# A hybrid attention block on one core: weights' neighbours reordered, gates kept ahead, branch sums added in DRAM

## The chip, the cores and the metric

The kernel runs on one NeuronCore of a Trainium2 chip. The core has TensorE (PE in the profile, with its weight loads as PEld), VectorE (DVE), ScalarE (ACT), GpSimd (POOL) and SyncE (SP), which run side by side and meet at semaphores; data comes from DRAM by DMA, issued here by SP, ACT and POOL. TensorE writes its sums to PSUM, which has eight banks. The metric is the device time of one execution in microseconds, as the median of several runs.

## The reference, cut to what matters

The input is 512 tokens of width 2048. One RMSNorm feeds one wide projection; its columns are split among three branches and three gates. All is float32.

```python
h = rms_norm(x, norm_g);  proj = h @ w_in
conv_y = b_gate * causal_depthwise_conv(c_gate * u, conv_w)          # 1024 channels
o_conv = (conv_y * silu(conv_z)) @ w_conv_out
mla_y  = mla_attention(...)      # 16 heads: low-rank q and kv, QK-norm, rotary part, block-causal mask
o_mla  = (mla_y * silu(mla_z)) @ w_mla_out
mem_y  = memory_attention(...)   # 4 heads of width 256 over 256 memory tokens, QK-norm
o_mem  = (mem_y * silu(mem_z)) @ w_mem_out
merged = sigmoid(g_conv) * o_conv + sigmoid(g_mla) * o_mla + sigmoid(g_mem) * o_mem
x = x + merged @ w_o
```

## The kernel before

Every product is made of three matmuls: an operand is split into a rounded part and its remainder (`split`, `weights`, `pair_split`: a copy on ScalarE gives the high half `whi`, a subtraction on VectorE the low half `wlo`), and `mm3` (L158 to L163) multiplies high by high, high by low, low by high.

Two kinds of product share one stream of weights. Dense products (`dense_units`) step through a weight matrix in chunks of two blocks of 128 rows; a unit is one `mm3`. Panel products (`panels`, `panel_steps`) use seven products in place of eight (Strassen's scheme in Winograd's form) on pairs of blocks: a weight chunk is loaded as four quarters, `pair_weights` adds four sums to them (L263 to L265), then splits seven; the moving side is prepared the same way by `pair_sums` (L243 to L246) and `pair_split` (L249, L250). A panel has four chunks, its first two panels are interleaved so that the fourth chunks, which need pairs 6 and 7, come last.

`queue` holds the weight chunks of all products in the order of their use, and `take` (L172) hands out the next one. When chunk c is taken, the halves of chunk c+1 are made and chunk c+2 is loaded (with `ahead=2` one further each). Raw weights have three buffers, halves two; in the first stage a third pair of buffers (`staged_parts`) serves every third chunk.

The stages follow each other so: keys and values of the memory (32 steps, during which x is scaled and its pairs made), the main projection `w_h` in 60 panels, 8 rounds of heads two at a time, the convolution's output product, the memory attention, `w_mla_out` in 8 panels, `w_mem_out` as dense product, and `w_o` in 8 panels.

TensorE's order is that of the program text. In the rounds of heads the text is interleaved by strings: `ORDER_KV` and `ORDER_Q` say after how many units of the projection for the next pair of heads (`w`) a step of an attention stream follows. `A` and `B` are the older pair's two streams, `a` and `b` the newer's. A stream's steps are: transposes of keys, of queries, of the rotary part (first head of a pair only), four blocks of scores with softmax, four of transposed probabilities, and the product with the values. `ORDER_MEM` does the same for four memory heads. SP's order is that of the text, too. The order on VectorE, ScalarE and POOL comes from a planner with simulated times, except where `manual_schedule` says that it is the text's: for VectorE this holds for the first six panel chunks of the main projection.

Gates are computed in the main projection and kept in DRAM (`gdram`). Where an output product ends, its banks are multiplied by the gate. `conv_result` writes the first branch's share to `mgdram`, `finish_mla` adds the second's by an accumulating DMA, and `mem_pair` (L1231) does the third: it loads gate and sum into one buffer `mg`, multiplies (L1236), adds (L1237), and makes the pair for `w_o` (`pair_parts`).

Of the kernel before, what the change touches and what calls it, by code (L numbers as in the profile page):

```python
# [30 lines left out]
P = 128  # L31
# [20 lines left out]
ORDER_KV = "2w B B B w B w A 6w B w B B B 5w"  # L52
ORDER_Q = "a a a B a a a 4w a w b b 5w a 4w a w a a w"
ORDER_KV1 = "16w"
ORDER_Q1 = "4w a a 2w a 2w a a a w a w b b 4w a w a w a a"
ORDER_LAST = "a a a B a a a 4w a w b b", "5w a 4w a w a a w"
ORDER_TAIL = "b b b b a 7w b w b b b 4w b"
ORDER_MEM = "0 0 4w 1 1 4w 0 0 2 2w 1 1 3 3w 0 0 2 2 w 1 1 3 3 2w 2 2 3w 3 3 w 2 2 3 3"
# [49 lines left out]
def body(ctx, tc, a, out):  # L108
# [165 lines left out]
    def panel_steps(xp, e, tag, middle=None, tail=None):  # L274
# [235 lines left out]
    def staged_parts():  # L510
# [7 lines left out]
    parts_of_x = all_parts()  # L518
    for grp in range(4):
# [43 lines left out]
    for _ in parts_of_x:  # L563
        pass
    close_st()
# [76 lines left out]
    def rotary():  # L642
# [76 lines left out]
        def turned(tag):  # L719
# [4 lines left out]
            nc.gpsimd.dma_start(krdram, kr)  # L724
        later.append(turned)
        yield
# [288 lines left out]

# [365 lines left out]
```

## Time and profile before

| what | us |
|---|---|
| median of 3 runs (lowest, highest) | 2192.47 (2190.98, 2194.52) |
| the profiled execution | 2187.3 |
| its span from first to last instruction | 2185.5 |
| TensorE busy | 2128.3 |
| VectorE busy | 1741.5 |
| ScalarE busy | 1003.8 |

The mean granted clock of TensorE over the span is 0.992. A row of a group of instructions reads: line, engine, operation, output and inputs by the program's names, shapes, count, then total busy time in us and the mean of one in ns, then idle time of the engine before them and what ended it. A row of waits reads: who waited, for whom, us in total, times, the longest. L12 is line 12 of the kernel before.

### The profile page before, as it was taken

The numbers are of one execution on the slowest core, as the hardware profiler recorded it, in microseconds if no ns is written. First come the engines' busy times: TensorE is split into PE (matmuls) and PEld (weight loads), VectorE is DVE, ScalarE is ACT, GpSimd is POOL, SyncE is SP. The second block draws the span as 40 slices with busy tenths as digits, with TensorE's granted clock in tenths as the row PEclk, the third lists the DMA queues.
The fourth block names the chain that finished last, engine by engine and source line by source line (L and its number), as shares of the span: only waits on it lengthen the run. The fifth ranks groups of instructions, "written<-read, shape, count | busy, mean of one in ns | idle before, by whom it ended". The sixth has DMA issues, their size and how long they took to land.

```text
span 2185.5 us, 38852 instructions
## 1 busy us (share of the span) xinstructions
PE 2128.3 (97%) x16040; PEld 2038.7 (93%) x16040; DVE 1741.5 (80%) x2764; ACT 1003.8 (46%) x1219; POOL 123.9 (6%) x173
## 2 busy tenths in 40 slices
PE   9989999999999999999999999999999999998799
PEld 8789999999999999999999999888888799987799
DVE  6986888888888888888888786888877688757787
ACT  6743444344334334444444444877764433323333
POOL 0000000000000000000000001221211100000000
PEclk9999999999999999999999999999999999999899
DMA  8633433333334334343444446222266765554343
GB/s 331 231 106 136 155 136 126 126 126 129 123 126 137 115 129 137 118 141 127 136 136 139 133 136 244 74 82 108 98 231 249 306 186 173 170 204 149 126 147 136
DMA packets 92289, 334.31 MB, mean 153 GB/s; under 512 B 10768, under 2 KB 11024, under 8 KB 90064
## 3 DMA queue, kind: packets, MB, share of 16 engines
q1 hardware_dynamic: 72000, 256.77, 34.4%
q0 software_dynamic: 11616, 51.12, 6.6%
q10 hardware_dynamic: 8496, 23.94, 3.1%
q8 instruction: 125, 2.05, 0.4%
q14 instruction: 52, 0.43, 0.1%
HBM read 273.34 MB, written 58.46 MB: 152 GB/s over the span
## 4 chain that ended last, share of the span: by engine, by line
PE 81%; DVE 8%; DMA 4%; issue 4%; ACT 2%; POOL 0%; SPq 0%; DVEq 0%; POOLq 0%; ACTq 0%
PE acc L161 14%; PE acc L162 14%; PE acc L163 14%; PE aux L163 11%; PE aux L162 11%; PE aux L161 11%; DVE wlo L269 3%; DMA raw<-in_w_mla_out 1%; DMA raw<-in_w_o 1%; DVE raw L263 1%; PE aux L978 1%; DMA sb<-gdram 1%; DMA raw<-in_w_h 1%; PE aux L961 1%; DVE wlo L155 0%
## 5 line engine op out<-in xcount | busy, mean ns | idle before, releaser
L268 ACT ACTIVATE whi<-raw 128x1792 fp32r<-128x1792 f32 x304 | 517.7, 1703 | 793.0 <-PE acc L162 352.8
L269 DVE TENSOR_TENSOR wlo<-raw,whi 128x1792 fp32r<-128x1792 f32 x304 | 614.3, 2021 | 194.2 <-ACT whi L268 193.7
L163 PE MATMUL aux<-xp,wlo 128*128 128x256 f32 (+1 forms) x1712 | 479.5, 280 | 5.0 <-DVE wlo L269 5.0
L161 PE MATMUL aux<-xp,whi 128*128 128x256 f32 (+1 forms) x1712 | 479.8, 280 | 1.0 <-ACT whi L268 1.0
L162 PE MATMUL aux<-xp,whi 128*128 128x256 f32 (+1 forms) x1712 | 480.0, 280 | 0.0
L163 PE MATMUL acc<-xp,wlo 128*128 128x256 f32 x1680 | 469.4, 279 | 3.4 <-DVE wlo L269 3.4
L162 PE MATMUL acc<-xp,whi 128*128 128x256 f32 x1680 | 469.8, 280 | 0.0
L161 PE MATMUL acc<-xp,whi 128*128 128x256 f32 x1680 | 469.3, 279 | 0.0
L163 PEld LDWEIGHTS aux<-xp,wlo 128*128 128x128 f32 (+1 forms) x1712 | 320.4, 187 | 5.6 <-DVE wlo L269 5.6
L161 PEld LDWEIGHTS aux<-xp,whi 128*128 128x128 f32 (+1 forms) x1712 | 321.4, 188 | 1.4 <-ACT whi L268 1.4
L162 PEld LDWEIGHTS aux<-xp,whi 128*128 128x128 f32 (+1 forms) x1712 | 320.9, 187 | 0.0
L163 PEld LDWEIGHTS acc<-xp,wlo 128*128 128x128 f32 x1680 | 314.6, 187 | 4.3 <-DVE wlo L269 4.2
L161 PEld LDWEIGHTS acc<-xp,whi 128*128 128x128 f32 x1680 | 315.6, 188 | 0.0
L162 PEld LDWEIGHTS acc<-xp,whi 128*128 128x128 f32 x1680 | 315.1, 188 | 0.0
L263 DVE TENSOR_TENSOR raw<-raw 128x512 f32<-128x512 f32 x304 | 208.0, 684 | 57.3 <-DMA raw<-in_w_h 29.8
L155 DVE TENSOR_TENSOR wlo<-raw,whi 128x1024 fp32r<-128x1024 f32 (+2 forms) x91 | 101.5, 1119 | 47.7 <-ACT whi L154 47.7
L154 ACT ACTIVATE whi<-raw 128x1024 fp32r<-128x1024 f32 (+2 forms) x91 | 88.9, 977 | 102.6 <-PE acc L162 41.5
L265 DVE TENSOR_TENSOR raw<-raw 128x256 f32<-128x256 f32 x304 | 127.7, 421 | 6.2
L264 DVE TENSOR_TENSOR raw<-raw 128x256 f32<-128x256 f32 x304 | 127.6, 420 | 5.7
L343 POOL TENSOR_TENSOR rs_r<-rs_t,mhalf 128x2 f32<-128x2 f32 (+2 forms) x71 | 69.5, 989 | 270.0 <-DVE rs_t L342 209.6
L161 PE MATMUL acc<-whi,blk 128*128 128x384 f32 (+1 forms) x224 | 84.8, 379 | 0.0
L163 PE MATMUL acc<-whi,blk 128*128 128x384 f32 (+1 forms) x224 | 80.9, 361 | 0.0
(359 smaller groups left out, 3900.9 us busy)
## 6 DMA issues: line engine op xcount, KB each, us to landing
raw<-in_w_h SPq DMA_DIRECT2D x240, 512.0 KB, 3.5
raw<-in_w_mla_out SPq DMA_DIRECT2D x32, 512.0 KB, 3.9
raw<-in_w_o SPq DMA_DIRECT2D x32, 512.0 KB, 3.7
raw<-in_w_mem_kv SPq DMA_DIRECT2D x31, 512.0 KB, 7.2
gdram<-e ACTq DMA_DIRECT2D x22, 512.0 KB, 2.8
raw<-in_w_ukv SPq DMA_DIRECT2D x16, 512.0 KB, 5.6
raw<-in_w_conv_out SPq DMA_DIRECT2D x16, 512.0 KB, 9.0
aadram<-z POOLq DMA_DIRECT2D x8, 896.0 KB, 4.1
```

The costliest lines, as they stand in the source:

```text
L154: act.activation(hi[:, cols], raw[:, cols], AF.Copy)
L155: vec.tensor_tensor(out=lo[:, cols], in0=raw[:, cols], in1=r32(hi[:, cols]), op=ALU.subtract)
L161: nc.tensor.matmul(o, lhsT=s[0], rhs=m[0], start=start, stop=False, skip_group_check=shared)
L162: nc.tensor.matmul(o, lhsT=s[0], rhs=m[1], start=False, stop=False, skip_group_check=shared)
L163: nc.tensor.matmul(o, lhsT=s[1], rhs=m[0], start=False, stop=stop, skip_group_check=shared)
L263: vec.tensor_tensor(out=f[:, 4:6], in0=f[:, 1:3], in1=f[:, 0:1].to_broadcast([P, 2, 256]), op=ALU.add)
L264: vec.tensor_tensor(out=f[:, 6], in0=f[:, 5], in1=f[:, 1], op=ALU.add)
L265: vec.tensor_tensor(out=f[:, 7], in0=f[:, 6], in1=f[:, 3], op=ALU.add)
L268: act.activation(hi, f[:, 1:8], AF.Copy)
L269: vec.tensor_tensor(out=lo, in0=f[:, 1:8], in1=r32(hi), op=ALU.subtract)
L343: pool.tensor_tensor(out=r, in0=t, in1=mhalf[:, :n], op=ALU.pow)
L961: nc.tensor.matmul(sb[:, :n], lhsT=qr[:, cols], rhs=krh[:, :n], start=False, stop=False)
```

## The change

- In the first stage the third pair of buffers serves chunks 0, 3, 6 and so on in place of 2, 5, 8; one more step uses `ahead=2`; one more raw chunk is loaded after the stage; VectorE's order is the text's from step 27 on until the sixth panel chunk.
- `take` can now carry other work: a list `fills`, of which one entry runs behind each chunk's weights. The x pairs 6 and 7 are made there, and in `w_o` the last two merged pairs and the results of a finished panel (`finish_o`).
- A panel's `middle` (loads for its end) stands at chunk 1 in front of its weights, not at chunk 2 behind them; the gate `sg` is loaded by POOL, not SP.
- In `rotary` the transposes of the shared key are put off by one step.
- The first three steps of a new pair of heads stand two units in front of the end of the keys' and values' product, not behind it; `ORDER_Q1` and `ORDER_MEM` are shifted by a few units.
- The convolution's gates are loaded a group ahead (`gate_blocks` is called on its own), and `my` has four buffers, not two.
- The third branch: gates lie in three places inside the tile of pair 7; the products with the gate stand right behind a group's matmuls (`gated`) and are added to `mgdram` by an accumulating DMA; the merged sum is loaded later (`merged`, partly into the tiles of pairs 5 and 6), and its sums and its split stand at fixed steps of the product (`steps_out`). VectorE's order is the text's from there until the ninth panel chunk of `w_o`.

```diff
-ORDER_KV = "2w B B B w B w A 6w B w B B B 5w"
-ORDER_Q = "a a a B a a a 4w a w b b 5w a 4w a w a a w"
+ORDER_KV = "2w B B B w B w A 6w B w B B B 3w a a a 2w"
+ORDER_Q = "B a a a 4w a w b b 5w a 4w a w a a w"
 ORDER_KV1 = "16w"
-ORDER_Q1 = "4w a a 2w a 2w a a a w a w b b 4w a w a w a a"
-ORDER_LAST = "a a a B a a a 4w a w b b", "5w a 4w a w a a w"
+ORDER_Q1 = "6w a a w a 2w a a a w a w b b 3w a w a w a a"
+ORDER_LAST = "B a a a 4w a w b b", "5w a 4w a w a a w"
-ORDER_MEM = "0 0 4w 1 1 4w 0 0 2 2w 1 1 3 3w 0 0 2 2 w 1 1 3 3 2w 2 2 3w 3 3 w 2 2 3 3"
+ORDER_MEM = "0 0 5w 1 1 5w 0 0 2 2w 1 1 3 2w 0 0 2 2 w 1 1 3 3 2w 2 2 2w 3 3 w 2 2 3 3"
...
+    fills = []
+    def begin(at):
+        if at < len(queue) and queue[at][1] is None:
+            queue[at][1] = queue[at][0]()
+            queue[at].append(next(queue[at][1]))
     def take(ahead=1):
-        for at, entry in enumerate(queue[:2 + ahead]):
-            if entry[1] is None:
-                entry[1] = entry[0]()
-                entry.append(next(entry[1]))
-            if at <= ahead and entry[2] is None:
+        for at, entry in enumerate(queue[:1 + ahead]):
+            begin(at)
+            if entry[2] is None:
                 entry[2] = next(entry[1])
+        begin(1 + ahead)
+        if fills:
+            fills.pop(0)()
         return queue.pop(0)[2]
...
         for c in range(nch):
+            if c == 1 and middle is not None:
+                middle()
             whi, wlo = take()
             if c == 2:
                 while later:
                     later.pop(0)("aux" if tag == "acc" else "acc")
-                if middle is not None:
-                    middle()
...
-                         (None, None, staged_parts), lambda c: memory_load(c + 1)))
+                         (staged_parts, None, None), lambda c: memory_load(c + 1)))
...
-                             ahead=lambda c: 2 if 0 < 8 * grp + c - 7 < 23 else 1):
+                             ahead=lambda c: 2 if 8 <= 8 * grp + c < 31 else 1):
...
+            if step == 27:
+                manual_dve.enter_context(tc.manual_schedule(engines={DVE}))
...
     for _ in parts_of_x:
         pass
+    begin(2)
...
+        yield
         later.append(turned)
-        yield
...
-    with tc.manual_schedule(engines={DVE}):
-        for step in range(6):
-            next(work)
-            if step == 0:
-                for i in (6, 7):
-                    xp.append(pair_tile(pxb, f"xp{i}"))
-                    x_load(i, etile())
-                late_parts = [x_pair(6), x_pair(7)]
-            elif step < 5:
-                for _ in range(1 + step % 2):
-                    next(late_parts[(step - 1) // 2])
+    for i in (6, 7):
+        xp.append(pair_tile(pxb, f"xp{i}"))
+        x_load(i, etile())
+        steps = x_pair(i)
+        fills += [lambda steps=steps: (next(steps), next(steps)), lambda steps=steps: next(steps)]
+    for _ in range(6):
+        next(work)
+    manual_dve.close()
...
-        return out
+        gates_of[grp] = out
...
-        for i, sg in enumerate(gate_blocks(grp)):
+        for i, sg in enumerate(gates_of[grp]):
...
-        run(ORDER_KV1 if grp == 1 else ORDER_KV, w=work, A=old[0], B=old[1])
         new = heads_of(grp - 1)
+        run(ORDER_KV1 if grp == 1 else ORDER_KV, w=work, A=old[0], B=old[1], a=new[0])
...
-                    if pg is not None:
+                    if grp > 0:
                         conv_result(grp, r)
+                    if grp == 2:
+                        gate_blocks(3)
...
+    gate_blocks(0)
     conv_result(0, results[0])
...
     pg, close_g = open_pool("gate", "right")
+    gate_blocks(1)
...
-            t = pq.tile([P, 2, S], F32R, tag="my", name="my", bufs=2)
+            t = pq.tile([P, 2, S], F32R, tag="my", name="my", bufs=4)
...
     pg, close_g = open_pool("gate2", "left")
+    gate_blocks(2)
...
-            nc.sync.dma_start(sgs[n], gdram[8 + n])
+            nc.gpsimd.dma_start(sgs[n], gdram[8 + n])
...
-    def mem_pair(n, banks):
-        t = pm.tile([P, 8, H], F32, tag="mg", name="mg", bufs=1)
-        nc.gpsimd.dma_start(two(t, 4), gdram[16 + n])
...
+    mplace = {0: 6, 1: 5, 2: 6, 3: 5, 5: 6}
+    def gate_load(n):
+        nc.gpsimd.dma_start(gates[n % 3], gdram[16 + n])
+    def merged(n):
...
         nc.gpsimd.dma_start(two(t), mgdram[n])
+        mgs[n] = t
+    def gated(n, banks):
+        gt = gates[n % 3]
         for i in range(2):
-            vec.tensor_tensor(out=two(t, 4)[:, i], in0=banks[i], in1=two(t, 4)[:, i], op=ALU.mult)
-        vec.tensor_tensor(out=two(t), in0=two(t), in1=two(t, 4), op=ALU.add)
-        yield
-        yield from pair_parts(t, xp[n])
+            vec.tensor_tensor(out=gt[:, i], in0=banks[i], in1=gt[:, i], op=ALU.mult)
+        nc.gpsimd.dma_start(mgdram[n], gt, accum_op=ALU.add)
+    def sums_out(n):
+        pair_sums(mgs[n])
+    def split_out(n):
+        x = place(n, f"xo{n}")
+        xp.append(x)
+        pair_split(mgs.pop(n)[:, 1:8], x)
+    steps_out = {9: ((merged, 0), (merged, 1), (gate_load, 3), (gate_load, 4)),
+                 14: ((sums_out, 0),), 15: ((split_out, 0),), 16: ((sums_out, 1),),
+                 17: ((split_out, 1), (merged, 2), (merged, 3), (gate_load, 5), (gate_load, 6)),
+                 22: ((sums_out, 2),), 23: ((split_out, 2),), 24: ((sums_out, 3),),
+                 25: ((split_out, 3), (merged, 4), (merged, 5), (gate_load, 7)),
+                 29: ((sums_out, 4),), 30: ((split_out, 4), (merged, 6)), 31: ((sums_out, 5),),
+                 32: ((split_out, 5),)}
...
             if n % 4 == 3:
-                next(pairs, None)
-        for _ in pairs:
-            pass
-        pairs = mem_pairs(done, banks)
+                step += 1
+                for do, k in steps_out.get(step, ()):
+                    do(k)
+        for i in range(width // 256):
+            gated(done + i, banks[2 * i:2 * i + 2])
...
     def finish_o(n, e):
+        fills.append(lambda: result(n, e))
...
-    for _ in work:
-        next(pairs, None)
+    merged(7)
+    fills += [lambda: None, lambda: sums_out(6), lambda: split_out(6), lambda: sums_out(7), lambda: split_out(7)]
+    for n, _ in enumerate(work):
+        if n == 8:
+            manual_dve.close()
```

More of the change, by code (lines that the diff above doesn't have):

```diff
@@ L1067, in conv_steps @@
                     results[grp] = r
[L1068 removed]
+                    if grp > 0:
                         conv_result(grp, r)
+                    if grp == 2:
+                        gate_blocks(3)
                 yield
     conv = conv_steps()
[L1073 removed]
     new = heads_of(NG - 1)
+    run(ORDER_KV, w=conv, A=old[0], B=old[1], a=new[0])
     run(ORDER_LAST[0], w=conv, A=old[0], B=old[1], a=new[0], b=new[1])
@@ L1226, in body, with place @@
     px, close_x = open_pool("xo", "right")
-    xp = [pair_tile(px, f"xo{i}") for i in range(NP)]
     pm, close_m = open_pool("merge", "right")
     pam2, close_am2 = open_pool("actm2", "left")
-    def mem_pair(n, banks):
-        t = pm.tile([P, 8, H], F32, tag="mg", name="mg", bufs=1)
-        nc.gpsimd.dma_start(two(t, 4), gdram[16 + n])
+    manual_dve.enter_context(tc.manual_schedule(engines={DVE}))
+    xp = []
+    def place(n, name):
+        return px.tile([P, 2, 7, H], F32R, tag=f"xo{n}", name=name, bufs=1)
@@ new lines, in body @@
+    gplace = r32(place(7, "gt")).rearrange("p a s n -> p (a s n)")
+    gates = [gplace[:, 1024 * i:1024 * (i + 1)].rearrange("p (f n) -> p f n", f=2) for i in range(3)]
+    mplace = {0: 6, 1: 5, 2: 6, 3: 5, 5: 6}
+    def gate_load(n):
+        nc.gpsimd.dma_start(gates[n % 3], gdram[16 + n])
+    mgs = {}
+    def merged(n):
+        if n in mplace:
+            t = r32(place(mplace[n], "mg")).rearrange("p a s n -> p (a s n)")[:, :2048]
+            t = t.rearrange("p (s n) -> p s n", s=8)
+        elif n < 7:
+            t = pm.tile([P, 8, H], F32, tag="mg", name="mg", bufs=1)
+        else:
+            t = pe.tile([P, 8, H], F32, name="mg7")
@@ L1249, in body @@
         late_blocks.append(t)
-    pairs = iter([])
-    done = 0
+    for n in range(3):
+        gate_load(n)
+    done, step = 0, 0
     for tag, width in (("acc", 512), ("aux", 512), ("acc", 512), ("aux", 256), ("aux", 256)):
@@ L1280, in finish_o, with result @@
     def finish_o(n, e):
+        fills.append(lambda: result(n, e))
+    def result(n, e):
         xr = xrs[n]
```

6 lines of the change are left out of this document (2 added, 4 removed).

## The prediction

> **What bounds the kernel now.** I read the page first, then the waits of TensorE, then the busy time of each engine in a stretch for each stage.
>
> ```profile
> span 2185.5 us, 38852 instructions
> PE 2128.3 (97%) x16040; PEld 2038.7 (93%) x16040; DVE 1741.5 (80%) x2764; ACT 1003.8 (46%) x1219; POOL 123.9 (6%) x173
> ```
>
> TensorE is busy 97% of the span, so 57.2 us of idle time, and the time in which its clock is halved, are all that this change can win; it removes no matmul. The profiled execution took 2187.3 us beside its span of 2185.5; the median of the runs is 2192.47, 5.2 above it. I sum savings against the profiled one and take them off the median.
>
> Waits of TensorE, longest first (total us, times, longest):
>
> ```profile
> PE aux L161 <- DVE mg L1236: 15.0, 2, 14.4
> PE aux L163 <- DVE wlo L269: 8.3, 8, 2.2
> PE acc L163 <- DVE wlo L269: 7.2, 8, 1.6
> PE acc L161 <- DVE mg L1236: 5.7, 1, 5.7
> PE aux L163 <- DVE wlo L155: 4.7, 3, 2.8
> PE aux L961 <- DVE qr L948: 2.3, 7, 0.3
> ```
>
> Stretches by stage (length, then busy us and count of PE, PEld, DVE, ACT, POOL; granted clock; DMA share; GB/s):
>
> ```profile
> 100.00:175.00 75.00, 66.18 (x501) 63.46 (x500) 64.34 (x88) 33.80 (x29) 1.46 (x4) 0.95 0.38 132
> 175.00:1000.00 825.00, 825.00 (x7011) 824.80 (x7011) 682.77 (x939) 343.12 (x264) 8.67 (x15) 1.00 0.39 129
> 1340.00:1640.00 300.00, 295.06 (x1667) 262.14 (x1666) 242.74 (x700) 220.16 (x533) 69.66 (x81) 1.00 0.35 128
> 1640.00:1700.00 60.00, 58.47 (x323) 49.76 (x322) 40.16 (x87) 26.52 (x64) 8.82 (x16) 1.00 0.71 255
> 1700.00:1762.00 62.00, 55.71 (x292) 47.77 (x291) 45.72 (x48) 27.82 (x20) 7.03 (x13) 0.94 0.75 285
> 1800.00:1910.00 110.00, 107.74 (x897) 106.07 (x897) 86.39 (x114) 38.50 (x28) 4.24 (x5) 1.00 0.58 176
> 1910.00:1980.00 70.00, 69.32 (x306) 56.87 (x304) 40.33 (x47) 19.62 (x18) 5.35 (x10) 1.00 0.52 180
> 1980.00:2045.00 65.00, 42.93 (x254) 38.61 (x255) 45.59 (x60) 19.26 (x14) 3.92 (x8) 0.84 0.39 138
> 2004.00:2008.00 4.00, 2.99 (x14) 2.99 (x15) 3.66 (x7) 0.00 (x0) 0.00 (x0) 0.57 0.65 221
> 2037.00:2043.00 6.00, 6.00 (x32) 6.00 (x33) 4.10 (x6) 1.70 (x1) 0.00 (x0) 0.57 0.00 0
> ```
>
> The reader is to see where the loss lies. From 175 to 1000 us TensorE never idles. The seam from the memory branch's product into `w_o` (1980 to 2045) loses 65 - 42.93 = 22.1 us, and the halved clock costs 0.43 x 2.99 + 0.43 x 6.0 = 3.9 more while matmuls run: 26 us. The start of the main product (100 to 175) loses 8.8 idle and about 0.05 x 75 = 3.8 of clock. Memory attention and the start of `w_mla_out` lose 1.5 + 6.3 idle and 0.06 x 62 = 3.7 of clock. The heads lose 4.9, the `w_mla_out` panels 2.3. So the change has five places to win or lose in, and the seam is as large as the other four.
>
> **The change, part by part.** Units of work first. A 256-column matmul takes 825 / 7011 = 0.118 us, so a panel chunk (42 of them) 4.94 us; a 512-column one 69.32 / 306 = 0.227, so a step of 12 takes 2.72.
>
> *The seam.* Before, each output pair goes through one buffer `mg`: load gate and sum, two products out of PSUM, add, sums, split, and only then may the next pair load.
>
> ```profile
> POOL mg L1233 <- DVE xo L250: 103.7, 7, 20.1
> DVE mg L1236 <- DMA mg<-gdram: 17.8, 6, 4.1
> L250 DVE TENSOR_TENSOR xo<-mg,xo 128x1792 fp32r<-128x1792 f32 x8 | 16.2, 2023 | 8.9 <-ACT xo L249 8.9
> L1237 DVE TENSOR_TENSOR mg<-mg 128x1024 f32<-128x1024 f32 x8 | 9.8, 1220 | 0.9 <-DMA mg<-mgdram 0.8
> L155 DVE TENSOR_TENSOR wlo<-raw,whi 128x512 fp32r<-128x512 f32 x8 | 5.4, 683 | 0.0
> L1236 DVE TENSOR_TENSOR mg<-aux,mg 128x512 f32<-128x512 f32 x8 | 5.1, 685 | 9.1 <-DMA mg<-gdram 9.1
> L269 DVE TENSOR_TENSOR wlo<-raw,whi 128x1792 fp32r<-128x1792 f32 x304 | 614.3, 2021 | 194.2 <-ACT whi L268 193.7
> L263 DVE TENSOR_TENSOR raw<-raw 128x512 f32<-128x512 f32 x304 | 208.0, 684 | 57.3 <-DMA raw<-in_w_h 29.8
> L264 DVE TENSOR_TENSOR raw<-raw 128x256 f32<-128x256 f32 x304 | 127.6, 420 | 5.7
> mgdram<-sg POOLq DMA_DIRECT2D x7, 512.0 KB, 8.5
> mg<-mgdram POOLq DMA_DIRECT2D x6, 512.0 KB, 5.0
> ```
>
> The PSUM banks wait for that queue of pairs, and `w_o` needs the banks: that is the 14.4 and 5.7. After, gates lie loaded in three places, the two products (2 x 0.685 = 1.37) follow the matmuls at once, the result is added in DRAM by an accumulating DMA, and the sum comes back later. VectorE loses 8 adds of 1.22; POOL gains 8 accumulating DMAs, behind which the next loads stand. A round trip is 1.37 + 8.5 + 5.0 = 14.9 us; from a pair's last matmul (step 8) to its sums (step 14) lie 6 x 2.72 = 16.3, so it is just covered; for pair 4 five steps are left, 13.6, and VectorE stands about 1.3 there, about 1 of it reaching TensorE.
>
> VectorE's order is now written by hand, so I add it up. Sums of a pair or of a raw chunk: 0.68 + 2 x 0.42 = 1.53; a split or a chunk's `wlo` 2.02. From step 28's end: products of pair 6 1.37, `wlo` 0.68, sums 4 1.53, `wlo` 0.68, split 4 2.02, `wlo` 0.68, raw sums 1.53, sums 5 1.53, first `w_o` `wlo` 2.02: 12.0. TensorE is there after 4 x 2.72 = 10.9: it waits 1.1. Then raw sums 1.53, split 5 2.02, products of pair 7 1.37, `wlo` 2.02: 19.0, against 12.0 + 4.94 = 16.9: 2.1 more. Later chunks fit: 3.55 of weights and a piece of at most 2.02 from `fills` in 4.94, with the debt worked off in chunks 2 and 6. With pair 4 that leaves 1 + 1.1 + 2.1 = about 4. Saving 26 - 4 = 22. Ends: 26 (all of it) and 10 (the debt is not worked off, some 2 us in each of six chunks more).
>
> *The start.* `parts` put the spare buffers on chunk 0, 3, ... 30, so the first panel's halves no longer wait for chunk 30's; `begin(2)` loads the third panel chunk earlier; x pairs 6 and 7 come in `fills` right behind the first weights.
>
> ```profile
> DVE wlo L269 <- ACT whi L268: 4.6, 2, 4.3
> L484 DVE TENSOR_TENSOR e<-e,xscale 128x1024 f32<-128x1024 f32 x2 | 2.4, 1218 | 0.0
> ```
>
> VectorE stood 4.3 us there with the pairs' work still to come; now that work fills it. In the written order, from step 27 (13.6 before the first panel): three plain `wlo` of 1.22 (as L1237's shape), split of pair 4 2.02, scaling 1.22, raw sums 1.53, sums 1.53, first `wlo` 2.02: 12.0, ready in time if VectorE comes without debt. Then 1.53 + 2.02 + 1.53 + 2.02: 5.5 after the first chunk's start against 4.94; the following four chunks add 3.55 and 2.75 (scale and sums) or 2.02 in turn against 4.94. Waits by that running sum: 0.6, 0, 0.4, 1.3, 0.7. With 1 us of debt and the row-sum matmuls' 1 us about 5, and one halved-clock window (1.7) in place of two: 12.6 - 6.7 = 6 saved. Ends 11 and -3 (the same waits, each queued behind a pair's split).
>
> *The heads.* Three transposes of the new head pair move two units ahead of the keys' product's end, so that the splits are ready for the scores.
>
> ```profile
>   PEld aux L961: 4.0, 8
>   PEld acc L161: 1.1, 6
> ```
>
> The first line (who waited for L948) is what is aimed at. The second (who waited for L863) says that the queries' product already waits a little, six times, for the keys' banks to be emptied; coming 1 us sooner, it finds them later still. ScalarE's splits keep their number. Ends 4.9 and -4; I take 2.5, half of the loss. The later yield in `rotary` only moves a small block: 0.
>
> *Memory attention and `w_mla_out`'s start.*
>
> ```profile
> 1702.26 12.03 DMA sb<-gdram
> ACT my L130 <- DMA amdram<-my: 8.6, 2, 5.7
> SPq L1178 <- DVE my L132: 18.4, 2, 9.8
> ```
>
> The first is on the chain that ended last: the product waits for its gate, `wlo` is queued behind it on VectorE. After, gates are on their way a group earlier, on POOL behind `amdram` writes. With `my` four deep ScalarE no longer waits 8.6, so SP's `xm` loads, and the raw weights behind them, start some 7 us sooner. Of 11.5 lost I keep 4 (a first transpose's wait, one jam of splits, one clock window): 7.5 saved; ends 11 and 2. In the panels `sg` moves from SP to POOL and a chunk earlier: SP's raw loads are freed of its waits; 1 of 2.3 saved, ends 2 and -2.
>
> ```profile
> mg<-gdram POOLq DMA_DIRECT2D x6, 512.0 KB, 3.7
> sg<-gdram SPq DMA_DIRECT2D x8, 512.0 KB, 4.4
> ```
>
> The same 512 KB landed no later from POOL than from SP. The Trainium skill speaks against the move: "SBUF — State Buffer", section "SBUF: two separate sides", says that VectorE in some modes shuts GpSimd out of a shared port, so that a DMA issued by GpSimd waits for its descriptors. These two rows show nothing of it; by the rule `sg` would win nothing and the sum would be 1 us less. "TensorE: Matmul & The Clock Gate", section "The HAM clock gate", has the clock halve after about 3.4 us of idleness; around 100 to 175 no single wait is over 2.2 and the clock still fell to 0.95, so the trace disagrees; by the rule the start would keep 1.7 less.
>
> Sum: 22 + 6 + 2.5 + 7.5 + 1 = 39 us. 2192.5 - 39 = 2153.5.
>
> **Rivals.** (a) VectorE is the bound at the seam and at the start, since the hand-written order lets a late piece hold up weights: savings 10 and 0 there, others as above: 21, so 2171. For it: 12.0 + 1.53 + 2.02 = 15.6 us of VectorE work in the last 10.9 of the memory product. Against: before, it did the same and 9.8 more. (b) Slower: the accumulating round trip. In the written order each group's sums stand in front of the weights. A trip T stops TensorE by about T - 19 in two groups (16.3 plus one step of cover), T - 14 in the third and T - 20 for pair 7: 4T - 72. It eats the 39 from T = 28 on; at 30 it costs 48, and the time is 2153.5 + 48, about 2201. Against: landings of 8.5 and 5.0 in stretches that are as full. (c) The heads' move does nothing, the wait only changing from scores to banks, all else holding: 2156. (d) All ends are good: 26 + 11 + 4.9 + 11 + 2 = 55, so 2138.
>
> **How the numbers follow.** The forecast with (c), savings of 27 to 48: 0.66. (a), 10 to 27: 0.20. (d) and beyond: 0.06. (b), slower: 0.05. The remaining 0.03: gains and new waits cancel. A change of 0.2% (4 us) is about what this measurement can tell. Faster 0.92, the same 0.03, slower 0.05. The range from 2138 (d) to 2176 (beyond (a)) leaves out some 2 in 10.
>
> **What would show it.** Right: waits for L1236's successor gone, granted clock 0.95 or more from 1960 to 2020, no `sb<-gdram` on the chain, VectorE's 4.3 wait at 110 gone. Wrong: VectorE waiting for `mg<-mgdram` by several us with `wlo` behind it; the wait of L961 replaced by one of acc L161 on L863; new waits for `wlo` L269 above 2 us in the first five chunks of either panel product.

## The result and the profile after

The changed kernel took 2176.16 us (median; 2174.03 to 2177.73), the kernel before 2191.72 beside it on the same chip: a ratio of 0.9931, with an interval of 0.991 to 0.9952. That is 15.6 us faster where 39 were forecast, and 22.7 above the predicted 2153.5. The profiled execution took 2174.03.

The page of the changed kernel, and its waits of TensorE (us in total, times, longest):

```profile
span 2172.3 us, 38860 instructions
PE 2125.0 (98%) x16040; PEld 2035.9 (94%) x16040; DVE 1734.1 (80%) x2756; ACT 1005.4 (46%) x1219; POOL 135.8 (6%) x189
```

```profile
PE acc L163 <- DVE wlo L278: 14.1, 14, 2.0
PE aux L163 <- DVE wlo L278: 10.1, 11, 3.0
PE acc L161 <- DVE mx L975: 3.0, 6, 0.5
PE aux L968 <- DVE z L1010: 2.7, 6, 0.6
...
PE aux L163 <- DVE wlo L155: 1.5, 1, 1.5
PE acc L161 <- ACT kn L873: 1.2, 6, 0.2
```

The two bank waits of 14.4 and 5.7 us are gone, with nothing on L1278 (L1236's successor) in their place. What is left is one wait: `wlo` L278 (L269 before) took 15.5 us and takes 24.2. The heads have three new waits, on L975, on L1010 and, with 1.2 us, on `kn` L873, while the one on `qr` has shrunk from 2.3 to 0.2. (For `kn` L863 and this product, the kernel before has only waits of weight loads, PEld, and none of a matmul.)

Stretches of the changed kernel (columns as before; stages now start up to 7 us earlier):

```profile
100.00:175.00 75.00, 66.07 (x502) 63.10 (x501) 65.80 (x87) 34.72 (x30) 1.47 (x4) 0.97 0.39 131
1975.00:2040.00 65.00, 60.45 (x420) 55.75 (x419) 54.28 (x70) 24.87 (x19) 4.50 (x7) 0.97 0.56 163
2037.00:2075.00 38.00, 29.15 (x229) 28.13 (x228) 30.53 (x44) 10.60 (x7) 0.00 (x0) 0.97 0.42 143
```

The seam idles 4.6 us instead of 22.1, at a clock of 0.97 instead of 0.84. But right behind it, from 2037 to 2075, a new hole of 8.9 us has opened; the kernel before idles 2.0 us from 2045 to 2100. The panels of `w_mla_out` no longer idle at all (105.00 of the 105 us from 1800 to 1905 are busy); the start loses as much as it did.

To place the rest, I measured each stage from its first matmul to the next stage's, in both traces:

| stage | before | after | gained | forecast |
|---|---|---|---|---|
| main product `w_h` with its start | 1227.8 | 1229.9 | -2.1 | 6 |
| heads, convolution's output | 313.2 | 317.9 | -4.7 | 2.5 |
| memory attention, `w_mla_out` | 258.9 | 246.2 | 12.7 | 7.5 + 1 |
| `w_mem_out`, `w_o` | 272.9 | 265.7 | 7.2 | 22 |

The sum is 13.1, which is the difference of the two spans (2185.5 - 2172.3 = 13.2); the medians differ by 15.6, and the table places only what these two executions show. One correction belongs to the last two rows, and it is explained in the last section: TensorE ran `w_mla_out`'s later panels some 3.4 us faster in this execution, and before's `w_o` some 3.4 us faster in the other, for no reason that the edits give. Without that, the gains are 9.3 and 10.6.

### The profile page after: what moved, and what is told of

Same layout as the page of the kernel before. It is cut to its first block, busy times and chain, and to the rows that moved or that the text cites. A ratio compares the mean times of both kernels' runs of the same rounds, so it can differ in the third digit from the quotient of the medians.

```text
span 2172.3 us, 38860 instructions
## 1 busy us (share of the span) xinstructions
PE 2125.0 (98%) x16040; PEld 2035.9 (94%) x16040; DVE 1734.1 (80%) x2756; ACT 1005.4 (46%) x1219; POOL 135.8 (6%) x189
## 5 line engine op out<-in xcount | busy, mean ns | idle before, releaser
L278 DVE TENSOR_TENSOR wlo<-raw,whi 128x1792 fp32r<-128x1792 f32 x304 | 614.3, 2021 | 197.1 <-ACT whi L277 196.4
L161 PE MATMUL aux<-xp,whi 128*128 128x256 f32 (+1 forms) x1712 | 480.6, 281 | 0.0
L161 PE MATMUL acc<-xp,whi 128*128 128x256 f32 x1680 | 470.3, 280 | 0.0
L161 PEld LDWEIGHTS aux<-xp,whi 128*128 128x128 f32 (+1 forms) x1712 | 320.9, 187 | 0.0
L161 PEld LDWEIGHTS acc<-xp,whi 128*128 128x128 f32 x1680 | 315.2, 188 | 0.0
L155 DVE TENSOR_TENSOR wlo<-raw,whi 128x1024 fp32r<-128x1024 f32 (+2 forms) x89 | 100.5, 1129 | 66.7 <-ACT whi L154 64.4
L274 DVE TENSOR_TENSOR raw<-raw 128x256 f32<-128x256 f32 x304 | 127.9, 421 | 6.6
L161 PE MATMUL acc<-whi,blk 128*128 128x384 f32 (+1 forms) x224 | 86.0, 384 | 4.1 <-DVE mx L975 3.0
```

The costliest lines, as they stand in the source:

```text
L155: vec.tensor_tensor(out=lo[:, cols], in0=raw[:, cols], in1=r32(hi[:, cols]), op=ALU.subtract)
L161: nc.tensor.matmul(o, lhsT=s[0], rhs=m[0], start=start, stop=False, skip_group_check=shared)
L274: vec.tensor_tensor(out=f[:, 7], in0=f[:, 6], in1=f[:, 3], op=ALU.add)
L278: vec.tensor_tensor(out=lo, in0=f[:, 1:8], in1=r32(hi), op=ALU.subtract)
```

## The experiments

Line numbers are those of the changed kernel; kernels with an inserted line have them shifted by a few. "The changed kernel" without a number is the 2176.16 us above.

### The new hole in `w_o`

Two theories on the hole: raw weights come late because SP, which issues their loads, stands at the load of `xr`; or the order written out in the text makes each chunk's sums, copy and subtraction follow one another. First, `xr` is loaded by POOL:

```diff
-            nc.sync.dma_start(xrs[n].rearrange("p f n -> p (f n)"), a["xT"][:, n])
+            nc.gpsimd.dma_start(xrs[n].rearrange("p f n -> p (f n)"), a["xT"][:, n])
```

> The changed kernel with one line other: the residual xr of the last product is loaded by POOL's queue, not SP's. Theory 1 (SP stands 10.5 us in front of xr of panel 2, which needs the output of panel 0 to be written, and the raw weights queued behind come late): the waits between 2037 and 2072, 2.1 + 2.2 + 1.0 + 3.2 us, shrink to 2 or less, and the time falls by 5 to 7, to about 2170. Rival (VectorE is the bound there, two panels' ends together with the weights): the wait of SP goes, the waits for wlo stay, and the time stays within 2 of 2176.

Second, in the first nine chunks of `w_o` a raw chunk is loaded and summed one chunk further ahead, so that its sums no longer stand just in front of its own split:

```diff
-        begin(1 + ahead)
+        for at in range(1 + ahead, 2 + ahead + further[0]):
+            begin(at)
...
+    further[0] = 1
     for n, _ in enumerate(work):
         if n == 8:
             manual_dve.close()
+            further[0] = 0
```

> The changed kernel with raw chunks begun one further ahead in the first nine chunks of the last product, so that on VectorE a chunk's raw sums stand a whole chunk in front of its wlo. Theory 1 (in the order of the text a chunk's sums, ScalarE's whi and VectorE's wlo follow each other with nothing between that counts: 1.53 + 1.70 + 2.02 and gaps = 5.45 us for 4.94 us of TensorE): chunks without an extra piece fall to 4.94, the 0.4 us waits from 2004 to 2032 go where no piece stands, and the time falls by 2 to 3, to about 2173. Rival (VectorE's sum of work alone is the bound: 3.55 and a piece of 2.02 are 5.6 anyway): the 0.4 us waits stay in chunks with a piece and the time is the same within 1.

Third, the hand-written order of VectorE ends where `w_o` begins, and the planner orders it:

```diff
+    manual_dve.close()
-    for n, _ in enumerate(work):
-        if n == 8:
-            manual_dve.close()
+    for _ in work:
+        pass
```

> The changed kernel, but in the last product VectorE's order is the planner's from its first chunk on; the memory product before it keeps the order of the text. Theory 1 (the order of the text puts a chunk's raw sums directly in front of its wlo, which costs 0.5 us in each of nine chunks; a planner may put them a chunk ahead): the waits of 0.4 us from 2004 to 2032 go or come in fewer places, and the last product's stretch falls from 176.2 us by 3 or more. Rival (the work behind the first chunks, in whatever order, is the bound): the stretch stays within 2 of 176, since the same waits lie elsewhere.

Measured, with `w_o` from its first to its last matmul (176.2 in the changed kernel): `xr` on POOL 2173.03 us and 169.4 (ratio to before 0.992, 0.9899 to 0.9941); further ahead 2169.88 and 166.8 (0.9902, 0.9885 to 0.9918); planner 2175.15 and 174.6 (0.9927, 0.991 to 0.9943). None of the three intervals is clear of the changed kernel's 0.991 to 0.9952, so the traces have to decide.

Who waited in the changed kernel, VectorE first (1985 to 2075), then SP's queue (1960 to 2075):

```profile
DVE raw L272 <- DMA raw<-in_w_o: 7.1, 4, 3.8
DVE wlo L278 <- ACT whi L277: 5.0, 5, 1.9
```

```profile
SPq L1333 <- DMA out<-xr: 10.5, 1, 10.5
```

SP stood 10.5 us at `xr`, whose buffer an earlier result had to leave, and the raw chunks behind it reached VectorE up to 3.8 us late. The hole's single waits, counted from one matmul's start to the next (0.16 us above the profile's rows), are 1.1 and 2.1 us, then 2.2, 1.0 and 3.2. The first two, at 2038.6 and 2045.7, come ahead of the first late chunk (2048.9); in front of them VectorE makes the ends of two panels. With `xr` on POOL SP's row is gone, and the hole shrinks by the profile's rows from 8.8 us to 6.3, not to nothing: VectorE still stands up to 2.5 us for a raw chunk, and the longest wait of TensorE is 3.8. The waits ahead of the hole, 0.4 us in nearly every chunk, are still there in that run. They have another cause, which the timelines of VectorE and ScalarE in the changed kernel show (start, length, what; at the end idle time before and its cause):

```profile
2003.24 2.03 DVE L278 TENSOR_TENSOR wlo<-raw,whi 128x1792 fp32r<-128x1792 f32 x1 [1.91 <-ACT whi L277]
...
2008.70 2.03 DVE L278 TENSOR_TENSOR wlo<-raw,whi 128x1792 fp32r<-128x1792 f32 x1 [0.39 <-ACT whi L277]
...
2012.17 2.02 DVE L259 TENSOR_TENSOR xo<-mg,xo 128x1792 fp32r<-128x1792 f32 x1
2014.16 2.02 DVE L278 TENSOR_TENSOR wlo<-raw,whi 128x1792 fp32r<-128x1792 f32 x1
```

```profile
2006.96 1.71 ACT L277 ACTIVATE whi<-raw 128x1792 fp32r<-128x1792 f32 x1 [3.75 <-DVE raw L274]
```

From `wlo` to `wlo` lie 5.46 us: 2.03 for `wlo`, 1.53 for the next chunk's sums, 1.70 for the copy on ScalarE, which waits for those sums (its releaser is L274), and the gaps between them. VectorE is idle for part of it: 1.91 in a chunk without a piece of `fills`, 0.39 in one with sums. In a chunk with a split (L259 at 2012.17) its own work fills the 5.46. TensorE needs 4.94. So a delay, once there, is not worked off: it grows by about half a microsecond in each chunk. Begun one further ahead, the sums leave the circle, and what remains from 2004 to 2032 is 0.2 us in every second chunk, those with a split. Waits of TensorE from 1985 to 2110 in the changed kernel, then in that run:

```profile
PE acc L163 <- DVE wlo L278: 8.0, 7, 2.0
PE aux L163 <- DVE wlo L278: 4.0, 5, 3.0
```

```profile
PE acc L163 <- DVE wlo L280: 5.6, 6, 1.6
PE aux L163 <- DVE wlo L280: 0.7, 2, 0.5
```

With that edit TensorE's waits in this stretch, the copy's included, fall from 12.4 us to 6.5, the clock from 1985 to 2085 rises from 0.97 to 1.00, and TensorE's pace is the same: this cause is shown, with 9.4 us off the stage. The 6.8 us with `xr` on POOL are not all its own. TensorE's waits from 1985 to 2110 only fall from 12.4 to 10.5, and in that execution the end of `w_o` ran at the quicker pace of the last section. From 2085 to 2150, never idle, first the changed kernel, then that run:

```profile
2085.00:2150.00 65.00, 65.00 (x554) 65.00 (x553) 55.83 (x78) 24.11 (x18) 0.00 (x0) 1.00 0.47 164
```

```profile
2085.00:2150.00 65.00, 65.00 (x576) 65.00 (x575) 57.22 (x79) 24.78 (x18) 1.59 (x3) 1.00 0.50 162
```

From 2070 on that is worth some 3.5 us, so about 3 are left for SP. The two edits together (below) come to 166.5, no better than the second alone, so no run shows that `xr` on POOL adds anything to it. The part of the panels' ends in the hole was not tested alone. With the planner's order the waits only lie elsewhere (7.7 and 3.9 in total). From 1975 to 2090 VectorE stands 2.3 us there for ScalarE's copy, but 12.2 for raw chunks and 4.1 for `mg<-mgdram`, so that run has other causes and says little on the written order.

### The heads

The three strings of the move as before:

```diff
-ORDER_KV = "2w B B B w B w A 6w B w B B B 3w a a a 2w"
-ORDER_Q = "B a a a 4w a w b b 5w a 4w a w a a w"
+ORDER_KV = "2w B B B w B w A 6w B w B B B 5w"
+ORDER_Q = "a a a B a a a 4w a w b b 5w a 4w a w a a w"
...
```

> The changed kernel with the three strings of the rounds of heads as before: a new pair's transposes again behind the end of the keys' product. Theory 1 (the move itself costs: VectorE and ScalarE make the new pair's splits in front of the emptying of the keys' banks, so the scores wait for the value product's bank and the queries' product for the keys' banks): the stretch from the first keys' product to the convolution's first matmul goes back from 264.6 us to about 259.3, the waits for z L1010 and mx L975 go, and the time falls by some 5, to about 2171. Rival (the stretch is longer through the planner's other choices or through the shifted first round): it stays near 264 and the time near 2176.

It took 2172.17 us (0.991, 0.9894 to 0.9925), and the heads 258.9 us in place of 264.6, where before had 259.2. So the move costs about 5 us. Only the keys' and the queries' transposes moved, the rotary part's behind the end as before:

```diff
-ORDER_KV = "2w B B B w B w A 6w B w B B B 3w a a a 2w"
-ORDER_Q = "B a a a 4w a w b b 5w a 4w a w a a w"
+ORDER_KV = "2w B B B w B w A 6w B w B B B 3w a a 2w"
+ORDER_Q = "a B a a a 4w a w b b 5w a 4w a w a a w"
...
```

> The changed kernel with only the transposes of keys and queries two units ahead of the end of the keys' product; those of the rotary part stand behind it, as before. Theory 1 (each split that VectorE makes in front of the keys' banks delays their emptying by its 0.7 us): two of three splits stand in front, the stretch of the heads is between 258.9 and 264.6, near 262. Rival (the interrupted product is what costs, whatever stands in the gap): it stays at 264.

It took 2168.37 us in its single run, and the heads 257.9. My theory that each of the three splits costs its share fell: two of them cost nothing, and the loss comes with the third. VectorE in one round, in the kernel before and then in the changed one:

```profile
1440.22 0.68 DVE L948 TENSOR_TENSOR qr<-aux,qr 64x512 fp32r<-64x512 f32 x1
1440.93 0.69 DVE L1000 TENSOR_TENSOR z<-aux,z 128x512 f32<-128x512 f32 x1
1441.54 1.65 DVE L134 SCALAR_TENSOR_TENSOR vl<-acc,kr__97,vh 128x256 fp32r<-128x256 f32 x4
```

```profile
1440.54 0.68 DVE L958 TENSOR_TENSOR qr<-aux,qr 64x512 fp32r<-64x512 f32 x1
1441.26 0.74 DVE L866 TENSOR_REDUCE ss<-sq 128x2 f32<-128x256 f32 x2
...
1442.05 0.95 DVE L155 TENSOR_TENSOR wlo<-raw,whi 128x768 fp32r<-128x768 f32 x1
...
1443.44 0.68 DVE L1010 TENSOR_TENSOR z<-aux,z 128x512 f32<-128x512 f32 x1
...
1446.22 0.48 DVE L134 SCALAR_TENSOR_TENSOR vl<-acc,kr__97,vh 128x256 fp32r<-128x256 f32 x1
```

Before, `z` (which empties a bank for the scores) and the four `vl` (which empty the banks of keys and values) follow `qr` at once, and the last ends 2.3 us behind it. After, `qr` has overtaken the sums of squares of the last two banks; `z` starts 2.2 us behind `qr`'s end, and the last `vl` ends 5.5 us behind it, among the maxima of the scores. Those are the waits on L1010 and L975 in the list at the top.

But `qr` itself has moved. Counted from the end of the last matmul of the keys' and values' product (1436.7 and 1440.6 in these rounds), the last `vl` ends 6.5 us later in the kernel before, 6.1 in the changed one and 5.3 with only two moved; the queries' product first writes to these banks 6.1, 4.5 and 5.2 us later, in all three nearly the same in every round. So with three moved TensorE asks 1.5 us sooner for banks that come only 0.4 sooner, and with two 0.9 sooner for banks that come 1.2 sooner. The order on VectorE can account for the 0.8 between 6.1 and 5.3, the sooner asking for the rest; no run changes the order alone. TensorE's longest wait in sum from 1340 to 1600 in the kernel with only two moved:

```profile
PE aux L971 <- DVE qr L958: 2.2, 7, 0.3
```

The wait that the edit aimed at is back at its old size, and nothing else has come.

### The start of the main product

The five edits of the start undone (`staged_parts`, `ahead`, `begin(2)`, the order's beginning, the late pairs in `fills`):

```diff
-                         (staged_parts, None, None), lambda c: memory_load(c + 1)))
+                         (None, None, staged_parts), lambda c: memory_load(c + 1)))
...
-    begin(2)
...
```

> The changed kernel with the start as before: spare buffers on chunks 2, 5, 8, the planner's order up to the first panel, pairs 6 and 7 behind the panel chunks, no third raw chunk in advance. Theory 1 (the hand-written order gains the 2 us of the first panel chunk and loses them again in the next, since VectorE has no time left there): the main product's stretch goes from 1229.9 us to about 1228, and the time falls by 0 to 2. Rival (the start does win, as the prediction had it, and another place in the main product loses): the stretch from 100 to 175 us loses 4 us or more than now, and the time rises by 4.

It took 2177.44 us (0.9938, 0.9915 to 0.9961), the same as the changed kernel; the start's edits bring nothing. TensorE's waits from 100 to 175 in the kernel before and in the changed one:

```profile
PE aux L163 <- DVE wlo L269: 4.1, 2, 2.2
PE acc L163 <- DVE wlo L269: 2.7, 3, 1.5
```

```profile
PE aux L163 <- DVE wlo L278: 4.7, 3, 2.3
PE acc L163 <- DVE wlo L278: 3.2, 4, 1.6
```

The waits at 107 and 110 are gone and as much has come in the chunks behind. The circle of `w_o` is not what makes them. One of VectorE's waits from 100 to 175 in the kernel before, and two in the changed one:

```profile
DVE raw L263 <- DMA raw<-in_w_h: 4.1, 4, 1.7
```

```profile
DVE raw L272 <- DMA raw<-in_w_h: 6.1, 4, 2.9
DVE wlo L278 <- ACT whi L277: 0.4, 1, 0.4
```

For ScalarE's copy VectorE stands 0.4 us at the start; from 117 to 139 it is never idle, with 5.4 to 6.2 us from `wlo` to `wlo`. So the first five waits of TensorE, 4.0 us, are VectorE's own load. The last two, 2.3 at 145.4 and 1.6 at 152.2, follow raw chunks that come 2.9 and 2.0 us late, and they stood in the kernel before as well, with 2.2 and 1.5. I had taken it for the circle, so I let the raw chunks run one further ahead here as well (together with `xr` on POOL, the same in `w_o`, and the heads' strings back):

```diff
+    further[0] = 1
     for _ in range(6):
         next(work)
     manual_dve.close()
+    further[0] = 0
```

> As the kernel with four edits, but the start is that of the changed kernel, with raw chunks begun one further ahead there too (in the first six panel chunks). Theory 1 (at the start, too, it is the order sums, whi, wlo without distance that makes each chunk 5.45 us): the waits for wlo from 112 to 151 us, 9 us in sum in the changed kernel, fall to 5 or less, and it is 3 to 5 us faster than the kernel with the start as before. Rival (VectorE has no time left at the start, since each of the first chunks has a piece of 2.0 to 2.75 behind it: 3.55 + 2.4 = 6 us for 4.94): the waits stay at 8 to 10 and the time is the same within 2.

The start gained (the two rows above fell to 2.7 and 2.2, the main product to 1224.6 us), and in the way that VectorE's rows say: the last two waits are gone, the first five are still there, with 4.9 us, so the theory that the order makes them fell. But the run took 2171.45 (0.9894, 0.988 to 0.9909), since the heads grew to 271.0. TensorE's longest wait there:

```profile
PE aux L161 <- DMA blk<-latdram: 4.2, 1, 4.2
```

An edit at 110 us has made a block late at 1338 us. The text between them is the same; the planner decides there on its own simulated times, and I take it that those shifted, but I did not follow it further.

### Memory attention

Two buffers for `my` again:

```diff
-            t = pq.tile([P, 2, S], F32R, tag="my", name="my", bufs=4)
+            t = pq.tile([P, 2, S], F32R, tag="my", name="my", bufs=2)
```

> The changed kernel with two buffers of my, as before. Theory 1 (the four buffers are what lets ScalarE finish the last memory heads without standing for amdram's landing, so that xm and the raw weights behind it on SP start some 7 us sooner): the wait of ScalarE's my for amdram of some 8 us comes back, xm's loads start 5 to 8 us later in relation to the convolution's last group, and the stretch from the memory attention's first matmul to w_mem_out's first, 246.2 us now and 258.9 before, grows by 4 to 8. Rival (the gates loaded a group ahead are what freed VectorE's queue): the stretch grows by 2 or less.

The gates loaded where their product needs them, as before, with four buffers kept:

```diff
+        if grp > 0:
+            gate_blocks(grp)
         for i, sg in enumerate(gates_of[grp]):
...
-    gate_blocks(1)
...
-    gate_blocks(2)
```

> The changed kernel with the convolution's gates loaded where they are used, as before. Theory 1 (the early gates free VectorE's queue, where wlo stood behind a gate for 3.9 us and TensorE 2.8): the wait of sb comes back with a wait of TensorE of 2 to 3 us near the convolution's last group and a window of halved clock; memory attention and the convolution's end, 86.9 us now, 91.0 before, take 89 to 91. Rival (with my four deep the queues are early enough anyway): 86.9 stays within 1.

With two buffers the single run took 2180.16 us, with late gates 2175.03 (0.993, 0.991 to 0.9951). Memory attention took 89.2 and 88.5 us against 86.9 in the changed kernel and 91.0 before. With two buffers ScalarE (first row) and TensorE (second, 1640 to 1770) wait again, as the kernel before did (8.6 and 2.8 us there):

```profile
ACT my L130 <- DMA amdram<-my: 10.2, 3, 5.5
```

```profile
PE aux L163 <- DVE wlo L155: 1.6, 1, 1.6
```

In the other kernels, whose edits don't touch this part, the stage takes 86.9 to 88.5 us. So the late gates' 88.5 says nothing against those, and no wait for a gate came back to TensorE, against what I had expected; the two buffers' 89.2 is just outside, and their waits are back in the rows. Neither alone gives back the 4.1 us of the stage, and `w_mla_out` took 164.2 and 164.4 in these two runs, inside the 162.1 to 165.1 of the other experiments (the changed kernel's 159.3 is at the quicker pace). What stands is that the four buffers take a wait away; how the rest of this gain divides stays open.

### Together

What seemed to help, without what cost: the strings as before, the start as before, `xr` on POOL, raw chunks of `w_o` one further ahead.

> The changed kernel with four edits together: strings of the rounds of heads as before, the start as before, xr loaded by POOL's queue, and raw chunks begun one further ahead in the last product's first nine chunks. Theory 1 (the four act in different places and add): 2176 - 4 (heads) - 0 (start) - 3 to 6 (POOL's load and the further chunk, which overlap in the last product) = 2165 to 2169, and the last product's stretch is at most 166 us. Rival (what one edit frees the next stage waits for anyway): not faster than the best of the single edits, 2170.

It took 2162.2 us (0.9852, 0.9838 to 0.9866). The same with the two transposes moved, in place of all strings back:

> The changed kernel with four edits together: only the keys' and the queries' transposes two units ahead, the rotary ones behind the product's end as before; the start of the main product as before; xr loaded by POOL; raw chunks of w_o begun one further ahead. Theory 1 (the parts add up): against the run with all strings back and the same three other edits (2162.2 us), the heads take 257.9 us in place of 258.9, main product 1226 to 1229, memory attention 87, w_o 166 to 168: 2161 us, between 2157 and 2165. Theory 2 (the planner answers an edit far away, as when the raw chunks were begun further ahead everywhere and the heads grew to 271.0): the heads are not 257.9 but 262 or more, and the time is 2166 or more.

It took 2160.53 us (0.9872, 0.9856 to 0.9889; 2155.93 to 2164.85), with heads of 257.9 us as expected. Against the run above the intervals overlap, so the 1 us shows in the stage and not in the time. Both are faster than the kernel before and than the changed one.

## Why the prediction was wrong

Of its own steps, in their order:

- **The seam.** The removal itself came as forecast: of the 26 us there, about 4 stayed as waits (1.69 in the product's last steps, 0.61 at the boundary and 1.72 in the first chunk; the prediction had 1, 1.1 and 2.1), and some 1.7 more as a clock of 0.87 from 1992 to 2005, which it had left out. The step that failed is "Later chunks fit: 3.55 of weights and a piece of at most 2.02 from `fills` in 4.94, with the debt worked off". It added up VectorE's work as if VectorE were the only one in it. The circle runs through ScalarE's copy, 5.46 us long, and it can't work off a debt: in the chunks without a piece, where the debt was to go, VectorE stood 1.91 us for that copy (2003.24 and 2030.51), and the chunk took 5.4 all the same. From 2004 to 2069 the waits are 0.58, five times 0.4, 1.09, 2.11, 2.21, 1.04 and 3.19, together 12.2; 22 - 12.2 is 9.8, and 10.6 was measured. The hole from 2037 on wasn't listed at all. SP at `xr` has a part in it: `finish_o` now puts the result, and with it the buffer's release, a chunk later, and `middle` asks for the load a chunk earlier; no run separates these two.
- **The start.** Here the running sum for VectorE held: 4 us of waits were forecast in the first chunks (3.0 and 1 of debt) and 1 at the row sums, and 4.0 and 1.0 came. The step that failed is taking the 12.6 that were lost there and leaving only these 5 and one clock window. It held the rest for gone, but 3.7 of it stood at 145.8 and 152.5 behind raw chunks that came late, and these waits are 3.9 now. So 8.9 us remain. The main product as a whole took 1228.4 to 1230.5 us in the runs that have this start unchanged (1225.2 in the one with late gates, which ran 130 us of it at the quicker pace), so the -2.1 of this one execution is no more than "no gain", and the edits undone give the same time.
- **The heads.** "I take 2.5, half of the loss", between 4.9 and -4; measured -4.7. The step that failed is this choice: the end of -4 had about the right price, and half of its reason. TensorE does come sooner, by 1.5 us, but the banks are not "later still"; they come 0.4 sooner. The sign named for it showed: the wait for `qr` fell from 2.3 to 0.2, and TensorE now waits 4.2 for these banks (3.0 on L975 and 1.2 on L873) and 2.7 for `z`. The line "PEld acc L161: 1.1, 6", read as the queries' product waiting already, was of weight loads alone; no matmul waited there before.
- **Memory attention and `w_mla_out`.** 8.5 forecast, 9.3 measured. The chain that ended last can't be asked for `sb<-gdram`, since in the changed kernel the profile follows it back to 1971.9 only; the 2.8 us that TensorE stood behind that gate are gone. The panels' 2.3 us of waits went whole where 1 was counted. With late gates the stage stayed inside the spread of the others, so that the gate was the wait that decided it, as the prediction had it, isn't borne out.
- **The rivals.** (a), VectorE as the bound at the seam and at the start (10 and 0 saved, 2171), came nearest, with 10.6 and -2.1; with the heads at -4.7 and not 2.5 its sum is 13.8, beside the 13.2 between the two executions. Its mechanism holds for the first chunks of the start and for the chunks of `w_o` with a split, not for the chunks without a piece and the late raw weights. (b) did not: the round trip is two products of 0.69, 6.5 and 6.0 us, 13.9 against 14.9 reckoned, and VectorE stood 2.8 us in all for `mg<-mgdram`, of which the 1.5 on `wlo` L155 at 1971.9 are what reached TensorE at most. (c) was too kind.

Rows of the DMA issues of the changed kernel (KB each, us to landing):

```profile
sg<-gdram POOLq DMA_DIRECT2D x8, 512.0 KB, 4.1
mgdram<-gt POOLq DMA_DIRECT2D x8, 512.0 KB, 6.5
mg<-mgdram POOLq DMA_DIRECT2D x8, 512.0 KB, 6.0
```

`sg` lands in 4.1 us from POOL, where it took 4.4 from SP. The Trainium skill ("SBUF — State Buffer", section "SBUF: two separate sides") has GpSimd's descriptors wait for VectorE instructions in a two-port mode, and says of `tensor_tensor`, which VectorE mostly runs there, that it has no such mode. So the rule did not speak against the move, as the prediction took it to, and the trace shows no loss.

## What to carry to other kernels

When work is written out by hand in a loop over engines, add up the longest circle through all of them (here sums, copy on another engine, subtraction: 5.46 us against TensorE's 4.94), not the busy time of the fullest engine: a loop whose circle is longer than the consumer's step never works off a delay, whatever its idle time says. Start a dependent step one iteration earlier, or keep it out of that loop. And of a loss that is to go, look at each wait for what it stood for, as the start shows. And when a transfer's buffer is released later, look at what else its queue has to issue behind it.

## What the runs showed of the hardware

TensorE runs the same 256-column matmul at more than one pace, and keeps one for hundreds of them. The same stretch, 2100 to 2150, never idle and at full clock, of the kernel before and of the changed one:

```profile
2100.00:2150.00 50.00, 50.00 (x443) 50.00 (x442) 44.95 (x64) 19.93 (x14) 0.00 (x0) 1.00 0.49 157
```

```profile
2100.00:2150.00 50.00, 50.00 (x426) 50.00 (x426) 42.37 (x59) 18.45 (x14) 0.00 (x0) 1.00 0.46 159
```

443 matmuls against 426 (or 427, by where the stretch begins) are 112.9 and 117.4 ns each. It isn't a matter of missing records: ScalarE's copies of whole chunks follow at 4.76 us in the one (2104.80, 2109.56, 2114.32) and at 4.94 in the other (2103.49, 2108.44, 2113.39). The quicker pace held in the changed kernel from 1812 us to the end of `w_mla_out` at 1902, in the kernel before from 2091 to the end, which is where the corrections of 3.4 us come from (90 us of `w_mla_out` or `w_o` by 0.18 in 4.76). A 512-column matmul takes 0.227 us in both, twice the quicker pace. With `xr` on POOL the pace changed 1.5 us behind a wait, at 2071; in the two stretches here it changed with no wait near. I put six pauses into the main product of the kernel with four edits ("Together"):

```diff
+        def go(tag):
+            b = bank(tag)
+            nc.tensor.matmul(b[:, :1], lhsT=ident, rhs=one, start=True, stop=True)
+            act.activation(bub[:, n:n + 1], b[:, :1], AF.Copy)
+            nc.tensor.matmul(b[:, 1:2], lhsT=ident, rhs=bub[:, n:n + 1], start=True, stop=True)
...
```

> The kernel with four edits, and in it six times (panels 11, 17, 23, 29, 35, 41 of the main product) a pause of TensorE: one tiny matmul, a copy of its result on ScalarE, another tiny matmul that needs the copy. It is to tell whether the two paces of TensorE that the traces show, one 256-column matmul each 117.7 or each 113.3 ns for the same instructions, are chosen by how TensorE comes out of a pause. Theory 1 (a pause picks the pace, which then holds until the next): after some of the six the matmuls run at 113.3 until the next pause, 0.74 us less per panel, and the main product is up to 25 us shorter less some 1 us per pause. Rival (the pace follows what else the core does, DMA or VectorE): the pace stays 117.7 through the main product as in all runs so far, and the time is 3 to 8 us longer.

It took 2172.46 us in its single run, and TensorE waited 9.9 us in the six pauses. The quicker pace never came, but a third one did. Ahead of the fifth pause (855.5), behind it, and behind the sixth (976.5):

```profile
800.00:850.00 50.00, 50.00 (x431) 50.00 (x430) 43.13 (x61) 23.46 (x18) 0.00 (x0) 1.00 0.37 119
870.00:920.00 50.00, 50.00 (x427) 50.00 (x426) 41.62 (x57) 18.88 (x13) 0.00 (x0) 1.00 0.38 127
985.00:1035.00 50.00, 50.00 (x431) 50.00 (x430) 45.35 (x90) 22.04 (x20) 4.69 (x3) 1.00 0.40 129
```

The pace changed behind two of the six pauses, by 1 ns a matmul, and not behind the others. What sets it is open. Until then, a difference of 3 or 4 us in one stage of one trace says nothing unless the pace was the same.

The clock, too, halves after less idleness than I would have thought. Two stretches of the changed kernel at the seam:

```profile
1989.80:1993.30 3.50, 1.50 (x8) 0.79 (x6) 3.05 (x5) 2.96 (x2) 0.09 (x1) 1.00 0.89 270
1993.30:1996.80 3.50, 3.50 (x18) 3.50 (x19) 3.43 (x5) 1.70 (x1) 0.00 (x0) 0.58 0.76 258
```

TensorE idled 2.0 us of the first, in waits of 0.4 and 1.6, and then ran at half its clock for some 3.4 us. The Trainium skill ("TensorE: Matmul & The Clock Gate", section "The HAM clock gate") has it fall after an idle window of some 3.4 us; the 3.4 us that it lasted agree with that window, the idleness ahead of it does not. At 110.6 in the kernel before it fell behind waits of 1.0 and 1.9 us, as the prediction said of the start. Its other fall there, at 171, decides nothing: ahead of it stand row sums of one column each, which the profile counts as busy.
